# Retention in matmuls of 64 rows, one copy of queries and keys, and tails at other times, in a hybrid streaming encoder

## The chip, the core and the metric

The kernel runs on one core of a Trainium2 chip. A core has a matrix engine (TensorE, PE in the profile; its weight loads are listed as PEld), a vector engine (VectorE, DVE), an engine for activation functions (ScalarE, ACT), a general one (GpSimd, POOL), one that issues most DMAs here (SyncE, SP), an on-chip memory (SBUF) of 128 partitions, and eight accumulator banks for PE's results (PSUM), each of 512 fp32 numbers on 128 partitions. The metric is the device time of one execution in microseconds.

## What is computed

One layer over 2048 prompt tokens and 64 sample tokens, width 1024. The input is RMS-normalized and projected by one matrix; three groups of heads use parts of the projection, each result is multiplied by a SiLU gate, and one output projection with the residual and a final RMS norm follows.

```python
h = rms_norm(x, norm_g)
proj = h @ w_in
# q, f, i, gate of HGRN2 (8 heads, 128/128); q, k, v, gate of retention (4 heads, 64/128); q, gate of attention (4 heads, 128)
o_hg = head_rms_norm(hgrn2_chunkwise(...), hg_norm_g) * silu(hg_gate)
o_rt = head_group_norm(retention_chunkwise(rq, rk, rv, ...), rt_norm_g) * silu(rt_gate)
o_xa = softmax(xq @ mem_k) @ mem_v * silu(xa_gate)
y = final_norm(x + concat(o_hg, o_rt, o_xa) @ w_out)

# retention, per head, within a chunk and from the state R of the chunks before
scores = (q @ k.T) * gamma ** abs(n - m)
o = scores @ v + (q * gamma ** (pos + 1)) @ R
R = gamma ** chunk * R + (k * gamma ** (chunk - 1 - pos)).T @ v
# head_group_norm: subtract the mean over the head's 128 values, divide by the root of the mean square
```

A retention head has queries and keys of 64 numbers and values of 128, so that two heads' queries fill 128 partitions.

## The kernel before

Tokens are worked in two groups (0 to 1023; 1024 to 2047 and the 64 sample tokens), each in blocks of 256 to 512 tokens. Per group: the gates of the retention heads, then the retention (`v_group` projects the values, `ret_group` the queries and keys, 128 tokens at a time, `gemm_tok`, L294), then the HGRN2 heads in two halves, then the attention heads (`xa_heads`). Gated results go to `mixT` in device memory. At the end the output projection (L1189) reads `mixT` back in quarters of 512 features, 128 tokens at a time.

The large projections are kept accurate by splitting each fp32 operand into a high and a low part (`split`: ACT rounds the high part, L240; DVE subtracts it, L241) and by three single-pass matmuls in place of an fp32 one. The small matmuls of the heads, among them retention's, are plain fp32, each of which is two PE instructions in the trace.

PE's and SP's instructions run in the order in which the program emits them. That order is made by hand: the GEMM loops advance a virtual clock (`pe(us)`) and after each of eight steps call `poll()`. A *tail* is a generator given to `task(class, generator, delay)`; when the virtual clock has passed its due time, `poll` runs it to its next `yield d`, which makes it due again d us later. Tails of one class stay in order. So the constants `D_...` say how much GEMM work is put between the steps of a tail. DVE, ACT and POOL follow a scheduler that ranks instructions by where they are emitted, and tails get a bonus. A matmul that comes too early for its operand, or for its PSUM bank, makes PE stand, with all that is behind it.

One retention tile has these steps in `retention_tail` (before's lines):

- L629: PE transposes q and k of the 128 tokens (4 transposes, bank `tr`). L633, L634: ACT copies q into `q2`, a zero-padded matrix with two heads on a block diagonal; L637 copies k; L639: DVE makes q times its decay, all from the same bank.
- after `D_RT1` = 2.5: L646, scores of two heads in one matmul (128 rows of k for two heads, 256 columns of `q2`; bank `scb`), twice; L650: DVE multiplies by the decay table, 128x512; L656: four matmuls of k-decay with v, for the state's update, two heads side by side in the output's partitions.
- after `D_RT2` = 3.5: L662, q-decay times R (R is block diagonal, 256 columns), not for the first tile; L666: scores times v added in the same bank, `ob`; L675: DVE updates R; L682: sums for the mean; L686: subtraction of the mean; L691: ACT squares; L236, L237: POOL makes the power -1/2; L694: DVE multiplies by it; L698: SP loads the gate.
- after `D_RT3` = 6: L702, four transposes, and DVE multiplies by the gate; the result is stored 4.5 later.

The HGRN2 tail has the same last steps (L572 and L575 matmuls into `ob`, squares, POOL's power, L583 multiply, `D_HG3` = 4, L590 transposes). The attention tail of a head is emitted `D_XA0` = 4 after its query: L750 scores into `ob`, softmax (L754 to L764), transposes L772, L794 values.

PSUM's eight banks: three for GEMM accumulators (`acc`), two for transposes (`tr`), one for retention's scores (`scb`), two for head results (`ob`), used in turn. A bank is given again when its readers are through.

## Time and profile before

| What | Value |
|---|---|
| device time, median of 3 runs | 1924.35 us (1923.58 to 1924.72) |
| the profiled execution's own time | 1926.11 us |
| its span, first to last instruction | 1924.3 us |
| mean granted clock of PE | 0.994 of full speed |
| PE busy | 1890.8 us, 98% |
| DVE, ACT, POOL busy | 1079.4, 585.6, 143.8 us |

The profile gives the busy time of each engine. "Granted clock" is the speed that the chip's throttle left to PE, with 1 as full speed. The chain of work that ended last is followed back from the last instruction. A row of the timeline has the start, the length from the first start to the last end, the engine, the line in the code, the operation with the names of its result and operands, its tile of PE's array or its form, the count of instructions, and in brackets how long the engine had been idle and which instruction released it. Grouped rows have the busy time and the mean of one in ns behind a bar, then the idle time before them by its releaser. Window rows have the length, then busy time (with the number of instructions) of PE, PEld, DVE, ACT, POOL, then the granted clock, the DMA share and GB/s.

In the trace, the first group's retention lies between 140 and 215 us, the second's between 862 and 965 us, the first attention head's tail near 641 us, and the output projection from about 1542 us on.

### The profile page before, as it was taken

To read this page: it belongs to the slowest core of one execution; us is meant where nothing else is said; L and a number is where in the kernel's file an instruction comes from. 1 tells how busy PE (TensorE), PEld (TensorE's weight loads), DVE (VectorE), ACT (ScalarE), POOL (GpSimd) and SP (SyncE) were. 2 spreads that over 40 slices of the span, in tenths; PEclk is the share of its full clock that TensorE was granted. 3 is DMA by queue.
4 is the path that set the end of the run, shared out by engine and by line. 5 is a ranking of instruction groups with operands and counts; after the bars stand their busy time and mean duration, and the time that the engine had idled before them with its cause. 6 is when DMAs were issued, how large, how long until landed. Compare 5 with 4: busy or idle time off the path is not lost.

```text
span 1924.3 us, 28262 instructions
## 1 busy us (share of the span) xinstructions
PE 1890.8 (98%) x10938; PEld 1614.2 (84%) x10938; DVE 1079.4 (56%) x2672; ACT 585.6 (30%) x1414; POOL 143.8 (7%) x335
## 2 busy tenths in 40 slices
PE   8999999999999999999999999999999999999998
PEld 7888788888888787987789999899998978888886
DVE  8527458763778547416728886388865652222222
ACT  7412233322232434412323332233333431111111
POOL 0001100000100100001101111011100000000000
PEclk9999999999999999999999999999999999999999
DMA  7511212111111413411311111111222352223322
GB/s 256 180 59 49 82 55 61 56 44 50 45 48 58 155 54 118 132 46 52 96 55 47 50 49 53 44 50 50 60 61 75 107 172 89 88 88 108 111 72 61
DMA packets 116743, 153.22 MB, mean 80 GB/s; under 512 B 13312, under 2 KB 79232, under 8 KB 116608
## 3 DMA queue, kind: packets, MB, share of 16 engines
q1 hardware_dynamic: 116608, 151.41, 25.8%
q8 instruction: 86, 1.41, 0.3%
q14 instruction: 49, 0.40, 0.1%
HBM read 117.69 MB, written 33.69 MB: 79 GB/s over the span
## 4 chain that ended last, share of the span: by engine, by line
PE 87%; DVE 5%; DMA 2%; ACT 2%; issue 1%; POOL 1%; SPq 0%; DVEq 0%; POOLq 0%; ACTq 0%
PE acc L249 40%; PE acc L1189 19%; PE acc L294 15%; PE ob L540 2%; PE ob L572 2%; PE ob L575 1%; PE scb L523 1%; PE ob L750 1%; PE acc L794 1%; PE acc L264 1%; PE tr L516 1%; ACT s L691 1%; PE tr L772 1%; PE tr L590 1%; DVE r L675 1%
## 5 line engine op out<-in xcount | busy, mean ns | idle before, releaser
L249 PE MATMUL acc<-hb,whi 128*128 128x320 f32 (+2 forms) x1696 | 410.2, 332 | 0.4 <-DVE hb L371 0.4
L249 PE MATMUL acc<-ha,whi 128*128 128x512 f32 x1120 | 354.1, 397 | 0.0
L249 PEld LDWEIGHTS acc<-hb,whi 128*128 128x128 f32 x1696 | 285.0, 190 | 22.1 <-DVE hb L371 0.6
L241 DVE TENSOR_TENSOR wlo<-wst,whi 128x1024 fp32r<-128x1024 f32 x115 | 139.7, 1222 | 261.0 <-ACT whi L240 260.0
L249 PE MATMUL acc<-hb,wlo 128*128 128x256 f32 (+2 forms) x848 | 277.4, 327 | 0.0
L249 PEld LDWEIGHTS acc<-ha,whi 128*128 128x128 f32 x1120 | 204.2, 189 | 40.3 <-issue 1.6
L249 PE MATMUL acc<-ha,wlo 128*128 128x512 f32 x560 | 219.4, 392 | 0.0
L240 ACT CAST whi<-wst 128x1024 fp32r<-128x1024 f32 x115 | 119.7, 1051 | 209.4 <-PE acc L249 169.2
L249 PEld LDWEIGHTS acc<-hb,wlo 128*128 128x128 f32 x848 | 160.5, 189 | 11.3
L294 PE MATMUL acc<-whi,ha 128*128 128x512 f32 x512 | 161.5, 396 | 0.0
L294 PE MATMUL acc<-whi,hb 128*128 128x512 f32 x512 | 159.9, 394 | 0.0
L249 PEld LDWEIGHTS acc<-ha,wlo 128*128 128x128 f32 x560 | 105.2, 188 | 23.4 <-DVE wlo L241 0.2
L1189 PE MATMUL acc<-whi,s 128*128 128x512 f32 x396 | 123.2, 390 | 1.3 <-ACT s L240 1.0
L294 PEld LDWEIGHTS acc<-whi,hb 128*128 128x128 f32 x512 | 94.5, 188 | 19.6 <-issue 1.2
L294 PEld LDWEIGHTS acc<-whi,ha 128*128 128x128 f32 x512 | 94.0, 189 | 19.3 <-issue 1.0
L294 PE MATMUL acc<-wlo,ha 128*128 128x512 f32 x256 | 100.0, 391 | 0.0
L294 PE MATMUL acc<-wlo,hb 128*128 128x512 f32 x256 | 99.8, 390 | 0.0
L1189 PE MATMUL acc<-hb,s 128*128 128x512 f32 x400 | 95.1, 394 | 0.0
L241 DVE TENSOR_TENSOR s<-mst,s 128x512 fp32r<-128x512 f32 (+1 forms) x64 | 40.4, 672 | 97.4 <-ACT s L240 97.4
L1189 PE MATMUL acc<-ha,s 128*128 128x512 f32 x400 | 93.7, 389 | 0.0
L1189 PEld LDWEIGHTS acc<-hb,s 128*128 128x128 f32 x400 | 76.2, 191 | 15.9
L1189 PEld LDWEIGHTS acc<-whi,s 128*128 128x128 f32 x396 | 74.2, 188 | 17.0 <-ACT s L240 1.3
(237 smaller groups left out, 2944.6 us busy)
## 6 DMA issues: line engine op xcount, KB each, us to landing
wst<-w_in_t SPq DMA_DIRECT2D x104, 512.0 KB, 4.0
mixT<-s SPq DMA_DIRECT2D x64, 256.0 KB, 4.4
mst<-mixT SPq DMA_DIRECT2D x30, 512.0 KB, 5.8
wst<-w_out_t SPq DMA_DIRECT2D x16, 512.0 KB, 4.1
xq<-x_prompt SPq DMA_DIRECT2D x18, 256.0 KB, 5.1
o_yp<-xq SPq DMA_DIRECT2D x18, 256.0 KB, 2.2
s<-mixT SPq DMA_DIRECT2D x16, 256.0 KB, 3.1
s<-x_prompt SPq DMA_DIRECT2D x16, 256.0 KB, 4.7
```

Source lines behind the costliest of these rows:

```text
L240: S.copy(hi, src)
L241: V.tensor_tensor(out=lo, in0=src, in1=hi.bitcast(F32), op=ALU.subtract)
L249: T.matmul(ps[:, 0:nt], w[a][:, kk, :], ht[b][:, kk, 0:nt], start=(n == 0), stop=(n == 23))
L264: T.matmul(ps[:, 0:nt], w[a][:, kk, :], ht[b][:, kk, 0:nt], start=(kk == 0 and a + b == 0), stop=(kk == KT - 1 and a == 1))
L294: T.matmul(ps[0:L, :], ht[b][:, kk, o:o + L], w[a][:, kk % 2, :], start=(n == 0), stop=(n == 23))
L516: T.transpose(trk[:, c * 128:(c + 1) * 128], kch[:, c * 128:(c + 1) * 128], ident)
L523: T.matmul(scb[32 * j:32 * j + 32, c * 128 + 32 * e:(c + 1) * 128], K[:, c * 128 + 32 * e:c * 128 + 32 * e + 32], Qe[:, c, E_OFF[e]:E_OFF[ ...
L540: T.matmul(db[:, c * 128:(c + 1) * 128], kT[:, c * 128:(c + 1) * 128], vt[c], start=True, stop=True)
L572: T.matmul(ob[:, c * 128:(c + 1) * 128], A[:, c * 128:(c + 1) * 128], vt[c], start=True, stop=first)
L575: T.matmul(ob[:, c * 128:(c + 1) * 128], qst[:, c * 128:(c + 1) * 128], st[c][0], start=False, stop=True)
L590: T.transpose(tro[:, c * 128:(c + 1) * 128], on[:, c * 128:(c + 1) * 128], ident)
L1189: T.matmul(ps, m[a][:, kk % 4], w[b], start=(n == 0), stop=(n == 16 * len(terms) - 1))
```

## The change

1. Scores: two heads are no longer in one matmul with a zero-padded operand. Each head has its own matmul over 64 rows (partitions 0 to 63 or 64 to 127), 128 columns. The even heads' scores go to `scb`, the odd ones' to a second bank, from `ob`.
2. q-decay times R: the same, one matmul of 64 rows per head, between the two pairs of scores-times-v matmuls. Even and odd heads have a bank each, one from `acc`, one from `tr`. (The sample tile takes four matmuls over 128 rows.)
3. One ACT copy takes q and k together out of the transposes' bank; q times decay goes into the buffers that held the padded queries.
4. DVE's multiplication of the scores, the sums for the mean and the subtraction of the mean are two instructions each, one per bank.
5. In the retention and the HGRN2 tail, the multiplication by POOL's power is emitted `D_PW` = 2 later than the power; the step behind it comes correspondingly sooner after it, so that the sum of both delays stays.
6. Head 0's attention tail is due 6.5 instead of 4 after its query where the block starts at token 0 or 1024; the tail of the last tile of each group's retention starts 2 later.
7. The first two of the four quarters for the first output tile are split ahead of the gate projection of the last attention head.

```diff
 (constants)
+D_PW = 2.0
+D_XA00 = 6.5
 ...
 (HGRN2 tail)
         rsqrt_small(rs[:, 0:nch], ss[:, 0:nch], nch, 1.0 / 128, 4 * EPS)
+        yield D_PW
         V.tensor_tensor(...)
-        yield D_HG3
+        yield D_HG3 - D_PW
 ...
-            task("rt", retention_tail(...), D_RT0)
+            task("rt", retention_tail(...), D_RT0 + 2.0 * (last_tile and o + L == nt))
 ...
 (retention_tail)
         q2 = q2b[(t // 128) % 2]
-        S.copy(q2[0:64, :, 0:L], trv[0:64, 0:2, 0:L])
-        S.copy(q2[64:128, :, 128:128 + L], trv[64:128, 0:2, 0:L])
-        kq = slot()
-        kqv = kq.rearrange("p (a b) -> p a b", a=4)
-        S.copy(kqv[:, 0:2, 0:L], trv[:, 2:4, 0:L])
+        qk = slot()
+        qkv = qk.rearrange("p (a b) -> p a b", a=4)
+        S.copy(qkv[:, :, 0:L], trv[:, :, 0:L])
         if not first:
-            V.tensor_tensor(out=kqv[:, 2:4, 0:L], in0=trv[:, 0:2, 0:L], in1=qdec[:, :, 0:L], op=ALU.mult)
+            V.tensor_tensor(out=q2[:, :, 0:L], in0=trv[:, 0:2, 0:L], in1=qdec[:, :, 0:L], op=ALU.mult)
         yield D_RT1
+        sc2 = (scb, obank())
         for p in range(2):
 ...
-                T.matmul(scb[:, p * 256:(p + 1) * 256], kqv[:, p, :], q2[:, p, :], start=True, stop=True)
-            pe(0.426)
+            for hh in range(2):
+                sl = slice(64 * hh, 64 * hh + 64)
+                T.matmul(sc2[hh][0:L, p * 128:p * 128 + L], qkv[sl, 2 + p, 0:L], qkv[sl, p, 0:L], start=True, stop=True)
+            pe(0.3)
 ...
+        for hh in range(2):
+            V.tensor_tensor(out=sdv[0:L, hh:4:2, 0:L], in0=sc2[hh]..., in1=dtab..., op=ALU.mult)
 ...
         yield D_RT2
-        ob = obank()
-        for p in range(2):
-            if not first:
-                T.matmul(ob[0:L, p * 256:(p + 1) * 256], kqv[:, 2 + p, 0:L], R[:, p, :], start=True, stop=False)
-                pe(0.426)
+        ob2 = (acc(), trp())
+
+        def av(p, start, stop):
             for hh in range(2):
                 h = 2 * p + hh
-                T.matmul(ob[0:L, h * 128:(h + 1) * 128], sdv[0:L, h, 0:L], v[0:L, h * 128:(h + 1) * 128], start=first, stop=first or hh == 1)
+                T.matmul(ob2[hh][0:L, p * 128:(p + 1) * 128], sdv[0:L, h, 0:L], v[0:L, h * 128:(h + 1) * 128], start=start, stop=stop)
                 pe(0.213)
+
+        def qr(p, start, stop):
+            for hh in range(2):
+                sl = slice(0, P) if sample else slice(64 * hh, 64 * hh + 64)
+                T.matmul(ob2[hh][0:L, p * 128:(p + 1) * 128], q2[sl, p, 0:L], R[sl, p, 128 * hh:128 * hh + 128], start=start, stop=stop)
+            pe(0.3)
+
+        av(0, True, first)
+        if not first:
+            qr(0, False, True)
+            qr(1, True, False)
+        av(1, first, True)
 ...
         rsqrt_small(rs[0:L], ss[0:L], 4, 1.0 / 128, EPS)
+        yield D_PW
         V.tensor_tensor(out=ccv, in0=ccv, in1=bc(rs...), op=ALU.mult)
 ...
-        yield D_RT3
+        yield D_RT3 - D_PW
 ...
 (attention)
-        task("xa", att_tail(h, tok0, nt, kv_p, kv_s, qh, ql, sh), D_XA0)
+        task("xa", att_tail(h, tok0, nt, kv_p, kv_s, qh, ql, sh), D_XA0 if h or tok0 % 1024 else D_XA00)
         poll()
+        if h == 3 and tok0 + nt == NTOK:
+            y_early.extend(y_split(raw0[0:2], P))
         psg = gemm_col(wg, ht, nt, rel)
 ...
 (output projection)
+        m = y_early + y_split(raw[2:], L) if o == 0 else y_split(raw, L)
```

In the changed program the line numbers are higher: L294 becomes L296, L629 L632, L662 L671, L666 L665, L702 L716, L249 L251, L572 L574, L575 L577, L590 L593, L750 L766. The order of PE's instructions for one retention tile in the middle of the first group, with the score and state-update steps of the tile behind it, was this (a row is the line, operation, result and operands, form and count of matmuls):

```order
L629 MATMUL tr<-cst,s 128x128 x4
L294 MATMUL acc<-whi,hb_548 128x512
...
L662 MATMUL ob<-r_113,s 128x256
L666 MATMUL ob<-v,s 128x128 x2
L662 MATMUL ob<-r_113,s 128x256
L666 MATMUL ob<-v,s 128x128 x2
L702 MATMUL tr<-cst,s 128x128 x4
L646 MATMUL scb<-q2b_139,s 128x256 x2
L656 MATMUL ob<-v,s 64x128 x4
```

And this is the same place after the change:

```order
L632 MATMUL tr<-cst,s 128x128 x4
L665 MATMUL acc<-v,s 128x128
L665 MATMUL tr<-v,s 128x128
L671 MATMUL acc<-r_113,q2b_138 128x128
L671 MATMUL tr<-r_113,q2b_138 128x128
...
L716 MATMUL tr<-cst,s 128x128 x4
L296 MATMUL acc<-whi,hb_548 128x512
...
L646 MATMUL scb<-s 128x128
L646 MATMUL ob<-s 128x128
...
L657 MATMUL ob<-v,s 64x128 x4
```

The four L671 of a tile stand between two pairs of L665, and results go to `acc` and `tr`. At this tile the transposes L632 stand directly ahead of that block and L716 directly behind it; three GEMM matmuls, which stood ahead of the block, now follow it.

The second place is the attention tail of head 0 in the first group, on PE. `Sn` and `abuf` are operands of the HGRN2 tail before it, and L249/L251 is a column-wise GEMM. Before, from the last L575 to the HGRN2 transposes L590 (nine L249 stand between L575 and L750, six behind it):

```order
L575 MATMUL ob<-Sn,s 128x128
L249 MATMUL acc<-ha_454,whi 128x512
...
L750 MATMUL ob<-s 128x256 x12
L249 MATMUL acc<-ha_454,whi 128x512
...
L590 MATMUL tr<-cst,s 128x128 x4
```

After (21 L251 stand between L577 and L766):

```order
L577 MATMUL ob<-Sn,s 128x128
L251 MATMUL acc<-ha_454,whi 128x512
...
L766 MATMUL ob<-s 128x256 x12
L593 MATMUL tr<-cst,s 128x128 x4
```

The attention scores moved behind 12 more GEMM matmuls, and now stand directly ahead of the HGRN2 transposes.

The third place is ACT, about the sample tokens' GEMM in the second group (L275 folds that GEMM's result). Before:

```order
L240 CAST whi<-wst 128x1024 x4
L633 COPY q2b_139<-tr 64x2x128
L634 COPY q2b_139<-tr 64x2x128
L691 ACTIVATE s,ss_8130<-s 128x128 x4
L275 COPY s<-acc 64x512
L637 COPY s<-tr 128x256
```

After:

```order
L242 CAST whi<-wst 128x1024 x4
L704 ACTIVATE s,ss_8233<-s 128x128 x4
L277 COPY s<-acc 64x512
L638 COPY s<-tr 128x512
```

The queries' copies, which stood ahead of the squares, are part of one copy with the keys, behind the squares and the fold.

More of the change, by code (lines that the diff above doesn't have):

```diff
@@ L620, in retention @@
                             in1=bc(kdec[L][0:L].rearrange("p (h o) -> p h o", o=1), [L, 4, 64]), op=ALU.mult)
-            task("rt", retention_tail(t, L, vt[c], r, kd, R[0 if L == 128 else 1], dtab), D_RT0)
+            task("rt", retention_tail(t, L, vt[c], r, kd, R[0 if L == 128 else 1], dtab), D_RT0 + 2.0 * (last_tile and o + L == nt))
             poll()
@@ L632, in retention_tail @@
         q2 = q2b[(t // 128) % 2]
-        S.copy(q2[0:64, :, 0:L], trv[0:64, 0:2, 0:L])
-        S.copy(q2[64:128, :, 128:128 + L], trv[64:128, 0:2, 0:L])
-        kq = slot()
-        kqv = kq.rearrange("p (a b) -> p a b", a=4)
-        S.copy(kqv[:, 0:2, 0:L], trv[:, 2:4, 0:L])
+        qk = slot()
+        qkv = qk.rearrange("p (a b) -> p a b", a=4)
+        S.copy(qkv[:, :, 0:L], trv[:, :, 0:L])
         if not first:
-            V.tensor_tensor(out=kqv[:, 2:4, 0:L], in0=trv[:, 0:2, 0:L], in1=qdec[:, :, 0:L], op=ALU.mult)
+            V.tensor_tensor(out=q2[:, :, 0:L], in0=trv[:, 0:2, 0:L], in1=qdec[:, :, 0:L], op=ALU.mult)
         yield D_RT1
+        sc2 = (scb, obank())
         for p in range(2):
-            if sample:
-                for hh in range(2):
-                    T.matmul(scb[0:L, p * 256 + hh * 128:p * 256 + hh * 128 + L], kqv[:, p, 0:L], q2[:, p, hh * 128:hh * 128 + L], start=True, stop=True)
-            else:
-                T.matmul(scb[:, p * 256:(p + 1) * 256], kqv[:, p, :], q2[:, p, :], start=True, stop=True)
-            pe(0.426)
+            for hh in range(2):
+                sl = slice(64 * hh, 64 * hh + 64)
+                T.matmul(sc2[hh][0:L, p * 128:p * 128 + L], qkv[sl, 2 + p, 0:L], qkv[sl, p, 0:L], start=True, stop=True)
+            pe(0.3)
         sd = slot()
         sdv = sd.rearrange("p (a b) -> p a b", a=4)
-        V.tensor_tensor(out=sdv[0:L, :, 0:L], in0=scb.rearrange("p (a b) -> p a b", a=4)[0:L, :, 0:L],
-                        in1=dtab.rearrange("p (a b) -> p a b", a=4)[0:L, :, 0:L], op=ALU.mult)
+        for hh in range(2):
+            V.tensor_tensor(out=sdv[0:L, hh:4:2, 0:L], in0=sc2[hh].rearrange("p (a b) -> p a b", a=4)[0:L, 0:2, 0:L],
+                            in1=dtab.rearrange("p (a b) -> p a b", a=4)[0:L, hh:4:2, 0:L], op=ALU.mult)
         db = obank()
@@ L681, in retention_tail @@
         mu = small(4, "mu")
-        V.tensor_reduce(out=mu[0:L], in_=ob[0:L].rearrange("p (a b) -> p a b", a=4), axis=AX.X, op=ALU.add)
+        for hh in range(2):
+            V.tensor_reduce(out=mu[0:L, hh:4:2], in_=ob2[hh][0:L, 0:256].rearrange("p (a b) -> p a b", a=2), axis=AX.X, op=ALU.add)
         V.tensor_scalar(out=mu[0:L], in0=mu[0:L], scalar1=1.0 / 128, scalar2=None, op0=ALU.mult)
@@ L685, in retention_tail @@
         ccv = cc[0:L].rearrange("p (a b) -> p a b", a=4)
-        V.tensor_tensor(out=ccv, in0=ob[0:L].rearrange("p (a b) -> p a b", a=4),
-                        in1=bc(mu[0:L].rearrange("p (a o) -> p a o", o=1), [L, 4, 128]), op=ALU.subtract)
+        for hh in range(2):
+            V.tensor_tensor(out=ccv[:, hh:4:2, :], in0=ob2[hh][0:L, 0:256].rearrange("p (a b) -> p a b", a=2),
+                            in1=bc(mu[0:L, hh:4:2].rearrange("p (a o) -> p a o", o=1), [L, 2, 128]), op=ALU.subtract)
         ss = small(4, "ss4")
@@ L1039, in layer_kernel, with y_split @@
     order = list(range(0, SEQ - P, P)) + [SEQ, SEQ - P]
-    def y_load(o, raw):
-        L = 128 if o < SEQ else DEC
-        src = io["x_prompt"][0, o:o + L] if o < SEQ else io["x_sample"][0]
-        if order.index(o) % 2:
-            x = a_buf
-        else:
-            xq = qep.tile([P, 4, 320], F32, tag="Qe", name="xq").rearrange("p a b -> p (a b)")
-            x = [xq[:, 0:512], xq[:, 512:1024]]
+    y_early = []
+    def y_split(raw, L):
         m = []
@@ L1058, in y_load @@
             m.append((hi, lo))
+        return m
+    def y_load(o, raw):
+        L = 128 if o < SEQ else DEC
+        src = io["x_prompt"][0, o:o + L] if o < SEQ else io["x_sample"][0]
+        if order.index(o) % 2:
+            x = a_buf
+        else:
+            xq = qep.tile([P, 4, 320], F32, tag="Qe", name="xq").rearrange("p a b -> p (a b)")
+            x = [xq[:, 0:512], xq[:, 512:1024]]
+        m = y_early + y_split(raw[2:], L) if o == 0 else y_split(raw, L)
         for i in range(2):
```

## The prediction

> **What bounds the kernel now.** I read the page first: busy time by engine, and the chain of work that ended last.
>
> ```profile
> span 1924.3 us, 28262 instructions
> PE 1890.8 (98%) x10938; PEld 1614.2 (84%) x10938; DVE 1079.4 (56%) x2672; ACT 585.6 (30%) x1414; POOL 143.8 (7%) x335
> PE 87%; DVE 5%; DMA 2%; ACT 2%; issue 1%; POOL 1%; SPq 0%; DVEq 0%; POOLq 0%; ACTq 0%
> s<-mixT SPq DMA_DIRECT2D x16, 256.0 KB, 3.1
> ```
>
> TensorE (PE) is busy 98% of the span and carries 87% of the chain. So two things move the end: PE's own work, and the few places where PE stands. Those are the second view, PE's waits by line (total us, times, longest; a line is that of the instruction, "<-" the one it waited for).
>
> ```profile
> PE tr L629 <- DVE s L617: 2.9, 2, 1.8
> PE scb L646 <- ACT s L637: 2.7, 1, 2.7
> PE acc L794 <- DVE s L241: 2.4, 2, 2.0
> PE tr L772 <- DVE s L764: 2.3, 1, 2.3
> PE ob L750 <- DVE s L583: 2.2, 1, 2.2
> PE tr L702 <- DVE s L694: 1.4, 2, 0.8
> PE ob L750 <- DVE Sn L563: 1.0, 1, 1.0
> PE acc L1189 <- ACT s L240: 1.0, 1, 1.0
> PE ob L656 <- DVE r L675: 0.6, 1, 0.6
> ```
>
> The third view is the granted clock by stretch. Behind a PE wait of over 2 us the clock falls to half for 3.4 us; the longer stretches hold one such fall each.
>
> ```profile
> 943.60:947.00 3.40, 3.40 (x17) 2.33 (x16) 2.84 (x6) 0.00 (x0) 0.46 (x1) 0.50 1.07 356
> 635.00:650.00 15.00, 12.64 (x64) 10.62 (x63) 6.08 (x17) 8.31 (x31) 3.95 (x11) 0.89 0.57 198
> 738.00:752.00 14.00, 11.69 (x50) 9.29 (x49) 12.59 (x24) 7.49 (x17) 0.00 (x0) 0.89 0.38 110
> 1538.00:1568.00 30.00, 26.34 (x132) 21.75 (x131) 21.14 (x39) 17.50 (x36) 0.00 (x0) 0.95 0.70 215
> 140.00:215.00 75.00, 71.23 (x406) 57.53 (x404) 54.52 (x114) 21.99 (x85) 8.62 (x14) 1.00 0.30 81
> ```
>
> The column after the five engines is the clock. Lost work is (1 - clock) x length: 3.4 x 0.50 = 1.7 us behind the 2.7 us wait, 15 x 0.11 = 1.65 behind the 2.2 us one at L750, 1.5 behind L772, 1.5 behind L794. So such a stall costs its length and about 1.6 us more. The last row is the retention of the first group: clock 1.00, VectorE (DVE) idle for 20 of 75 us.
>
> **Matmuls of 64 rows.** The timeline of PE inside one retention tile gives the spacings.
>
> ```profile
> 143.70 1.02 PE L646 MATMUL scb<-q2b,s 128*128 128x256 f32 x4
> 144.66 0.66 PE L656 MATMUL ob<-v,s 128*64 128x128 f32 x8
> 145.24 0.73 PE L294 MATMUL acc<-whi,ha 128*128 128x512 f32 x2
> 145.81 0.39 PE L294 MATMUL acc<-wlo,ha 128*128 128x512 f32 x1
> 146.93 0.39 PE L294 MATMUL acc<-wlo,ha 128*128 128x512 f32 x1
> 149.23 1.05 PE L666 MATMUL ob<-v,s 128*128 128x128 f32 x8
> 203.46 0.59 PE L662 MATMUL ob<-r,s 128*128 128x256 f32 x2
> 203.89 0.61 PE L666 MATMUL ob<-v,s 128*128 128x128 f32 x4
> ```
>
> An fp32 matmul is two PE instructions. A new one starts every (203.89-203.46)/2 = 0.215 us at 256 moving columns; about 0.27 us of each row's length is the drain of its last instruction. L666, 128 columns, full array: (1.05-0.27)/7 = 0.111 us apart. L656, also 128 columns but on half the array's output columns each: (0.66-0.27)/7 = 0.056. So two half-array matmuls do run at once in this program, for column halves. Row halves occur nowhere in this trace.
>
> Going into a half mode and out again costs: from 143.70 to 145.81 are 2.11 us, of which 4 x 0.215 + 8 x 0.055 + 2 x 0.23 = 1.76 is work (0.23 is a GEMM matmul of 512 columns: 10 start from 146.93 to 149.23). That leaves 0.35 for two switches, 0.18 each.
>
> Scores per tile: now 2 matmuls x 2 x 0.215 = 0.86 us. Then 4 matmuls of 128 columns, two at once: 4 x 0.11 = 0.44, and one switch more (row halves stand between full and column halves): 0.62, so -0.24 on 16 prompt tiles = -3.8. q·R: now 0.86, then 0.44 and two switches = 0.80, -0.06 on 15 tiles = -0.9. I take -4.5. Ends: row halves run one after another, and only the switches are added: 16 x 0.18 + 15 x 0.36 = +8.3. Both overlap and the switches vanish in weight loads: 31 x -0.43 = -13.3. I take the overlap because L656, the nearest row, is the same engine split the other way.
>
> [...]
>
> **One copy, halves on DVE, powers apart.** These rows are of the first group's retention, with the ACT copies.
>
> ```profile
> 146.68 0.37 ACT L633 COPY q2b<-tr 64x256 f32<-64x256 f32 x1 [4.39 <-PE tr L629]
> 728.91 0.59 ACT L361 COPY s<-tr 128x512 f32<-128x512 f32 x1 [3.73 <-PE tr L357]
> L694 DVE TENSOR_TENSOR s<-s,rs 128x512 f32<-128x512 f32 x7 | 4.8, 693 | 11.4 <-POOL rs L237 11.4
> L639 DVE TENSOR_TENSOR s<-tr,cst 128x256 f32<-128x256 f32 x7 | 2.9, 420 | 2.3 <-ACT s L637 2.3
> L675 DVE SCALAR_TENSOR_TENSOR r<-r,cst,ob 64x128 f32<-64x128 f32 x24 | 7.6, 343 | 0.1
> ```
>
> Three ACT copies of 0.37 (1.11) become one of 0.59: transposes to scores gets 0.5 us shorter. Three DVE operations on 128x512 (L650's scores, the reduction, the subtraction; 0.69 as L694) become pairs on 128x256 (0.42 as L639): +0.15 each, +0.45 us a tile, covered by the 20 us of idle. The normalizing multiply now stands in DVE's queue waiting for POOL's power, 11.4/7 = 1.6 us a tile, and everything behind it waits too (the q·decay multiply, r updates, weight splits). Two us of schedule between power and multiply take that wait out, so DVE's net is about -1.2 us a tile. The gate's DMA goes on SP's queue 2 us later as well, and weight fetches pass it; it lands in 3.1 us and has 4 left. The sample tile keeps four full matmuls; it is not counted.
>
> What PE waits in the retention, L646 aside, is 2.9 + 1.4 + 0.6 = 4.9 us, nearly all on DVE. Against that, the second half of each result now takes a transpose bank, of which there are two. So every tile passes that ring three times (L632, L665/L671, L716). Counting matmuls in the order (0.23 us for each of the GEMM's), 7 of the 17 tiles have only 1.3 to 2.9 us of PE work between the transposes and the next user of a bank that DVE or ACT must clear; DVE needs 4 x 0.34 + 4 x 0.42 = 3 us for updates, sums and subtractions. Ends: all 4.9 go, or 7 tiles wait 1 us each and the old waits stay, +7. I take -1, near the middle, as a quicker DVE and a busier ring oppose each other.
>
> **The wait before the sample tile** stands at 939.8 to 942.9.
>
> ```profile
> 941.92 0.56 ACT L275 COPY s<-acc 64x512 f32<-64x512 f32 x1
> 942.51 0.37 ACT L637 COPY s<-tr 128x256 f32<-128x256 f32 x1
> 942.93 1.47 PE L646 MATMUL scb<-q2b,s 128*128 128x256 f32 x4 [2.73 <-ACT s L637]
> ```
>
> ACT's order after the change still has the squares and the fold copy L275 ahead of the one copy; it ends at best 0.5 earlier, and PE's work ahead changes little. -0.5, the slow stretch stays. If other work comes ahead of it on PE, up to -2.7 - 1.7 = -4.4; if the 0.59 copy is late, +0.2.
>
> **Moved tails.** The attention tail behind head 0 and the HGRN2 tails:
>
> ```profile
> 643.51 1.65 PE L750 MATMUL ob<-s 128*128 128x256 f32 x6 [2.22 <-DVE s L583]
> 642.77 0.69 DVE L583 TENSOR_TENSOR s<-ob,rs 128x512 f32<-128x512 f32 x1 [2.38 <-POOL rs L237]
> 748.06 1.03 PE L772 MATMUL tr<-cst,s 128*128 128x128 f32 x6 [2.31 <-DVE s L764]
> 744.14 2.35 DVE L241 TENSOR_TENSOR wlo<-wst,whi 128x1024 fp32r<-128x1024 f32 x2
> 1560.89 1.14 ACT L240 CAST v<-wst 128x512 fp32r<-128x512 f32 x2 [2.42 <-DMA wst<-w_out_t]
> ```
>
> First head: L750 wants a bank that L583 clears, and L583 waits for the power. In the new order 21 instead of 9 GEMM matmuls stand between, 12 x 0.23 = 2.8 us later, which is over the 2.22 of the wait: -2.1, and its slow stretch -1.65, so -3.7. Head 0 of token 1024 passes the state work in the same way: -1, the whole of L563's wait. At 748.1 the order has DVE do L764 ahead of the two 1.2 us splits, but PE arrives 6 matmuls (1.4 us) earlier: -0.7 (ends 0 and -3.8). The multiply of the HGRN2 tail pushes its transposes one poll back, 0.7 us of GEMM between; hidden. Output stage: two of its first four splits are done beforehand, -1, the whole of L1189's wait; the wait at L794 hangs on the late w_out fetch (2.42) ahead of ACT's casts and stays.
>
> **Sum.** -4.5 - 1 - 0.5 - 3.7 - 1 - 0.7 - 1 = -12.4 us. The profiled execution took 1926.11, 1.8 above the median of the runs; the sum is a difference, so against the median: 1924.35 - 12.4 = 1912.
>
> **Rivals.** 1. *Row halves don't overlap* (the part that wouldn't do what it says): each half has its own 128-column weight load, and L656 overlapped loads of 64 columns only; L666 never shows 128-column loads nearer than 0.111. Then 4 x 0.22 = 0.86 a block as before, plus switches, +8.3 in place of -4.5: 1912 + 12.8 = 1925. For it: no row-half row at all; against: L656.
>
> [...]
>
> 2. *The stalls move*: the bank at the first head is waited for by the next user, the clock falls there all the same, the output stage waits for its third quarter instead. Then only the rows (-4.5), the retention (-1) and head 0 of token 1024 (-1) count: 1918. For it: POOL's power itself is not earlier; against: 12 matmuls cover it.
>
> 3. *The transpose ring binds* (slower): L716 or L632 meets a bank that DVE hasn't cleared, because a pair of splits of 2.35 us stands in DVE's queue. At 7 tight places of 2.35 us each, +16.5, and a stall of that length has drawn a slow stretch of 1.6 each time; with two of them more, +20. 1912 + 1 + 20 = 1933. Slower than before from (12.4 - 1 + 3.85)/7 = 2.2 us a place on. Against it: DVE loses its 1.6 us waits.
>
> **Chances.** The forecast 0.5, its own range 1905 to 1918; rival 1, 0.18; rival 2, 0.2; rival 3, 0.12. A difference under 0.2% (3.85 us) can't be told from none: same is 1920.5 to 1928.2. Forecast and rival 2 are faster but for 0.04 at the edge of it; rival 1 is the same, at 0.16, with 0.02 slower; rival 3 is slower. Faster 0.66, same 0.20, slower 0.14. The range goes from 1903 (the rows' term at its low end: 1912 - 13.3 + 4.5) to 1926, just over rival 1, leaving out rival 3 and little below.
>
> **What would show it.** Rows of 64: L646 and L671 should be about 0.055 us apart in the timeline; 0.11 proves rival 1. The idle ahead of L750's successor at 641 and ahead of the first L1189 successor gone, clock at 635 to 650 near 1.00. DVE's idle behind POOL at the two multiplies (11.4 us for seven) near 0. Waits of L632 and L716 on DVE of 2 us would be rival 3. The prediction fails outright if the first retention stage (75 us in the last window row) is not shorter by 2 us or more, or if a new wait over 2 us draws a slow clock.

## The result, and the profile after

The changed kernel takes 1912.05 us (median of 4 runs, 1909.42 to 1914.49) where the kernel before, in 4 runs, takes 1923.96: a ratio of 0.994 [0.9927, 0.9952]. A second measurement gave 0.9936 [0.9923, 0.9948]. The forecast was 1912, and the time is right. Most of its terms are of the right kind too, but their sizes are not, so that the sum is right by luck. Within about 2 us the gain comes from the moved delays, and not from the matmuls of 64 rows, which the forecast had as its largest term.

The page of the changed kernel (span; busy time by engine; the chain):

```profile
span 1907.6 us, 28493 instructions
PE 1882.3 (99%) x11066; PEld 1607.2 (84%) x11066; DVE 1081.8 (57%) x2723; ACT 576.3 (30%) x1380; POOL 144.2 (8%) x335
PE 87%; DVE 6%; DMA 2%; ACT 2%; issue 1%; POOL 1%; SPq 0%; POOLq 0%; DVEq 0%; ACTq 0%
```

PE is still the bound: busy for 8.5 us less (1890.8 before) in a span that is 16.7 us shorter. So half of what went from this profiled execution is standing time, and of the 8.5 about 3.4 are two stretches of slow clock fewer, in which matmuls take longer (in the kernel before, those of 512 columns start 0.43 us apart at half clock, 645.81 to 646.24 us, and 0.23 apart at full clock). (This execution, 1909.42 us, was the fastest of its kernel's four, and the one shown of the kernel before, 1926.11, was slower than all four timed beside it; that is why the spans differ by more than the 12 us of the medians.)

PE's waits after the change:

```profile
PE ob L766 <- DVE s L586: 3.1, 2, 2.1
PE tr L716 <- DVE s L708: 2.5, 4, 1.2
PE acc L810 <- DVE s L243: 2.4, 2, 1.7
PE scb L646 <- ACT s L638: 2.4, 1, 2.4
PE tr L632 <- DVE s L620: 1.4, 1, 1.4
```

L772's wait (now L788), the first L1189's (L1211) and L656's are gone from the head of the list. The attention scores (L766) still wait twice for the bank that L586 clears, once near 641 us as before and once at 1411 us, where L750 had waited 1.0 for something else. The transposes L716 wait more often.

The stretch at the first attention head now has a clock of 1.00, and so has the piece behind it; the one at the sample tile keeps its slow stretch ((1 - 0.88) x 14 = 1.7 us lost), and so does the output stage (the last row):

```profile
635.00:650.00 15.00, 14.04 (x71) 11.74 (x70) 6.85 (x16) 10.09 (x35) 4.62 (x13) 1.00 0.34 112
730.00:744.00 14.00, 14.00 (x73) 11.88 (x72) 13.84 (x28) 8.30 (x20) 0.00 (x0) 1.00 0.22 53
926.00:940.00 14.00, 11.56 (x77) 8.89 (x77) 11.04 (x23) 4.29 (x13) 2.15 (x2) 0.88 0.68 207
1522.00:1552.00 30.00, 27.61 (x141) 23.47 (x141) 22.18 (x42) 17.80 (x36) 0.00 (x0) 0.94 0.72 218
```

And these are the scores of a retention tile on PE, with the GEMM matmuls around them:

```profile
141.34 0.39 PE L296 MATMUL acc<-wlo,ha 128*128 128x512 f32 x1
141.66 0.37 PE L646 MATMUL scb<-s 64*128 64x128 f32 x1
141.66 0.37 PE L646 MATMUL ob<-s 64*128 64x128 f32 x1
141.87 0.27 PE L646 MATMUL scb<-s 64*128 64x128 f32 x1
141.88 0.27 PE L646 MATMUL ob<-s 64*128 64x128 f32 x1
141.98 0.27 PE L646 MATMUL scb<-s 64*128 64x128 f32 x1
141.99 0.27 PE L646 MATMUL ob<-s 64*128 64x128 f32 x1
...
142.30 0.66 PE L657 MATMUL ob<-v,s 128*64 128x128 f32 x8
142.89 0.72 PE L296 MATMUL acc<-whi,ha 128*128 128x512 f32 x2
143.45 0.39 PE L296 MATMUL acc<-wlo,ha 128*128 128x512 f32 x1
```

The two halves start within 0.01 us of each other: they run at once, and rival 1 is out. The first pair takes 0.21 us, the others 0.11 (the fourth, at 142.09, is left out above). From the end of the GEMM's matmul (141.34 + 0.23) to the next one at 142.89 are 1.32 us; before, 143.70 to 145.24 were 1.54. So a tile's scores save 0.22 us.

To see where time went I set the k-th projection matmul of one trace against the k-th of the other: these matmuls are the same in all versions, and the difference of their times, stage by stage, is what a stage gained or lost. Differences to the profiled execution before, in us; the stages are placed by the times of the kernel before. Slow stretches of the clock are 3.41 us at a granted clock of 0.50 in all traces (but for the one that runs into the program's end, of 6.55 us in the kernel before), or two or three of these in a row, each of which loses 3.41 x 0.50 = 1.7 us; in brackets stands how many more or fewer of them the stage has than before.

```
kernel        start     ret.1     635-850   ret.2     1417-30   output    all
after         -2.3      -1.8      -8.5 (-2) -3.0      +0.6      -1.8      -16.8
after_again   -1.3 (-1) -1.5      -9.0 (-2) -1.1 (+1) +0.6      -1.7      -14.0
rows_only      0.0 (-1) +0.3 (+1) -1.6      +2.3 (+2)  0.0      -0.2       +0.6
pw_only       -0.1 (-1)  0.0      -2.8 (-1) -0.2      -0.3      +0.1       -2.9
xa_only       -1.1       0.0      -5.3 (-1) +1.1      +2.1 (+1) +0.9       -2.4
y_only        -1.4 (-1)  0.0      -2.9 (-2) +2.0 (+2)  0.0      -3.1 (-1)  -5.5
sched_only    -0.7      -0.6      -9.3 (-2) -1.2      +0.6      -3.2 (-1) -14.1
rt_no_pw      -1.6 (-1) -0.1 (+1) -8.7 (-2) -2.3      +2.1 (+1) -3.2 (-1) -13.7
```

(Retention lies from 149 to 224 and from 851 to 966 us, the output stage's beginning from 1543 to 1633. What is missing to the sum lies between the stages, under 0.6 us each.) Single executions of a program differ by 1 to 2 us in a stage: the start by 1.0 between the two of the changed kernel, and the second retention by 1.1 between the kernel before and `xa_only`, whose retention is the same. So the start's 2.3 us are not shown to be the change's: in the second profile it is 1.3, and a missing slow stretch makes 1.7 of that.

The mean granted clock of every timed execution is on record as well. Its time times (1 - clock) is what it lost to the clock. Where "lost to the clock" and "the rest" are given below, they are means over all executions of a kernel; a difference of two such means is good to 1 to 2 us unless said otherwise.

### The profile page after: what moved, and what is told of

Read it like the earlier page. It is cut to its first block, busy times and chain, and to the rows that moved or that the text cites. A ratio compares the mean times of both kernels' runs of the same rounds, so it can differ in the third digit from the quotient of the medians.

```text
span 1907.6 us, 28493 instructions
## 1 busy us (share of the span) xinstructions
PE 1882.3 (99%) x11066; PEld 1607.2 (84%) x11066; DVE 1081.8 (57%) x2723; ACT 576.3 (30%) x1380; POOL 144.2 (8%) x335
## 4 chain that ended last, share of the span: by engine, by line
PE 87%; DVE 6%; DMA 2%; ACT 2%; issue 1%; POOL 1%; SPq 0%; POOLq 0%; DVEq 0%; ACTq 0%
PE acc L251 40%; PE acc L1211 18%; PE acc L296 15%; PE ob L542 2%; PE ob L574 1%; PE ob L577 1%; PE scb L525 1%; PE acc L810 1%; PE ob L766 1%; PE acc L266 1%; POOL rs L239 1%; PE tr L518 1%; PE tr L788 1%; ACT s L704 1%; PE tr L593 1%
## 5 line engine op out<-in xcount | busy, mean ns | idle before, releaser
L251 PE MATMUL acc<-hb,whi 128*128 128x320 f32 (+2 forms) x1696 | 409.0, 331 | 0.4 <-DVE hb L373 0.4
L251 PE MATMUL acc<-ha,whi 128*128 128x512 f32 x1120 | 353.0, 396 | 0.0
L251 PEld LDWEIGHTS acc<-hb,whi 128*128 128x128 f32 x1696 | 284.4, 189 | 22.0 <-DVE hb L373 0.6
L251 PE MATMUL acc<-hb,wlo 128*128 128x256 f32 (+2 forms) x848 | 276.9, 326 | 0.0
L251 PEld LDWEIGHTS acc<-ha,whi 128*128 128x128 f32 x1120 | 204.1, 188 | 40.5 <-issue 1.3
L251 PE MATMUL acc<-ha,wlo 128*128 128x512 f32 x560 | 219.1, 391 | 0.0
L251 PEld LDWEIGHTS acc<-hb,wlo 128*128 128x128 f32 x848 | 160.1, 189 | 11.2
L296 PE MATMUL acc<-whi,ha 128*128 128x512 f32 x512 | 161.4, 396 | 0.7 <-ACT v L1100 0.7
L296 PE MATMUL acc<-whi,hb 128*128 128x512 f32 x512 | 160.0, 394 | 0.0
L251 PEld LDWEIGHTS acc<-ha,wlo 128*128 128x128 f32 x560 | 105.1, 188 | 23.3 <-DVE wlo L243 0.2
L1211 PE MATMUL acc<-whi,s 128*128 128x512 f32 x396 | 122.9, 389 | 0.0
L296 PEld LDWEIGHTS acc<-whi,ha 128*128 128x128 f32 x512 | 93.9, 189 | 20.5 <-issue 1.2
L296 PEld LDWEIGHTS acc<-whi,hb 128*128 128x128 f32 x512 | 94.5, 188 | 19.6 <-issue 1.2
L296 PE MATMUL acc<-wlo,ha 128*128 128x512 f32 x256 | 100.0, 391 | 0.0
L296 PE MATMUL acc<-wlo,hb 128*128 128x512 f32 x256 | 99.9, 390 | 0.0
L1211 PE MATMUL acc<-hb,s 128*128 128x512 f32 x400 | 94.9, 393 | 0.0
L1211 PE MATMUL acc<-ha,s 128*128 128x512 f32 x400 | 93.7, 389 | 0.0
L1100 ACT COPY v<-acc 128x512 f32<-128x512 f32 x48 | 28.1, 586 | 204.4 <-PE acc L296 204.4
L1211 PEld LDWEIGHTS acc<-hb,s 128*128 128x128 f32 x400 | 76.0, 190 | 15.9
```

What stands on the lines that cost most here:

```text
L251: T.matmul(ps[:, 0:nt], w[a][:, kk, :], ht[b][:, kk, 0:nt], start=(n == 0), stop=(n == 23))
L296: T.matmul(ps[0:L, :], ht[b][:, kk, o:o + L], w[a][:, kk % 2, :], start=(n == 0), stop=(n == 23))
L1100: S.copy(v, ps)
L1211: T.matmul(ps, m[a][:, kk % 4], w[b], start=(n == 0), stop=(n == 16 * len(terms) - 1))
```

## The experiments

Each was timed in five rounds beside the kernel before, and profiled once. Ratios are to the kernel before. First the two halves of the change.

**Rows alone** (`rows_only`): all edits of the retention's matmuls, copies and DVE halves; none of the delays.

```diff
 (the changed kernel, less)
-        yield D_PW                     # both tails; D_HG3, D_RT3 whole again
-  ... D_RT0 + 2.0 * (last_tile and o + L == nt)
-  ... D_XA0 if h or tok0 % 1024 else D_XA00
-            y_early.extend(y_split(raw0[0:2], P))
```

> The kernel before with matmuls of 64 rows, the one copy and the halved DVE instructions, and no delay moved. If the row halves overlap as priced (a pair every 0.11 us, switches 0.18), it gains 4.5 us, and about 1 in the retention's waits: ratio 0.997, some 1918.5 us where the kernel before takes 1924; the waits at the first attention head (2.2 us and the slow stretch behind it) and behind it at 745 us stay. If the moved tails are the whole gain and the switches eat the overlap, 1923 to 1925, ratio 0.999 to 1.001.

Measured: 1925.97 us, 1.001 [0.9998, 1.0022]. No gain. The blocks on PE are as short as in the changed kernel, yet the retention stages are 0.3 and 2.3 us longer, with one and two slow stretches more. The 12 executions agree: 14.6 us are lost to the clock, where the kernel before, beside them, loses 9.3, while the rest is 3.3 us shorter (1911.4 against 1914.7). So most of what the rows save on PE does arrive, and slow stretches take it back. PE's waits there, of `rows_only`, first in the first group, then in the second:

```profile
PE acc L664 <- DVE s L650: 3.0, 1, 3.0
PE tr L631 <- DVE s L619: 0.5, 1, 0.5
...
PE tr L631 <- DVE q2b L639: 2.4, 1, 2.4
PE scb L645 <- ACT s L637: 2.3, 1, 2.3
PE tr L631 <- DVE s L619: 1.8, 1, 1.8
PE ob L656 <- DVE s L650: 0.6, 1, 0.6
```

The 3.0 us are a wait for the scores' multiplication (L650), which the kernel before did not have. Its timeline, around 203 us:

```profile
202.58 0.69 DVE L706 TENSOR_TENSOR s<-s,rs 128x512 f32<-128x512 f32 x1 [1.32 <-POOL rs L239]
203.19 0.42 DVE L650 TENSOR_TENSOR s<-scb,s 128x256 f32<-128x256 f32 x1
203.53 0.41 DVE L650 TENSOR_TENSOR s<-ob,s 128x256 f32<-128x256 f32 x1
203.75 0.48 PE L664 MATMUL acc<-v,s 128*128 128x128 f32 x2 [3.00 <-DVE s L650]
```

DVE works its queue in order here. The normalizing multiply of the tile before stands in it; DVE is idle for 1.32 us until POOL has the power, and only then come the scores that PE is waiting for, although their last matmul had started at 195.58 us. In the first group this only gathers the standing in one place: 3.7 us in sum with the small waits, where the kernel before stood 3.8 (L629's 1.8, L702's 1.4, L656's 0.6). But behind the 3.0 us a slow stretch follows at 204.1 us, and its 1.7 us are what the scores of the group's eight tiles save (8 x 0.22). In the second group PE also stands longer, 7.3 us against 4.6, and two more slow stretches follow.

**Delays alone** (`sched_only`): the kernel before with 128-row matmuls, and all four moves in time.

```diff
+D_PW = 2.0
+D_XA00 = 6.5
+        yield D_PW                     # both tails, taken off D_HG3 and D_RT3
+  ... D_RT0 + 2.0 * (last_tile and o + L == nt)
+  ... D_XA0 if h or tok0 % 1024 else D_XA00
+            y_early.extend(y_split(raw0[0:2], P))
```

> The kernel before with the moved delays alone (multiply 2 us behind its power, head 0's attention tail at 6.5, the last retention tail 2 later, the early split), and 128-row matmuls. By the sum of the prediction (-3.7 - 1 - 0.7 - 1, and some of the retention's waits) 1917 to 1918, ratio 0.9965. If the moved tails are the whole gain: 1912, ratio 0.994.

Measured: 1911.15 us, 0.9931 [0.9919, 0.9943], the same as the whole change; the rest is 8.0 us shorter, and 4.8 instead of 9.3 us are lost to the clock. So the rival wording, that the moved tails are the whole gain, is what holds within about 2 us. In the profile the changed kernel's retention is 0.9 to 1.2 us shorter than `sched_only`'s in the first group, and in the second 1.8 shorter in one execution and 0.1 longer in the other; in the total the difference disappears in the spread.

**Retention's multiply behind its power again** (`rt_no_pw`).

```diff
         rsqrt_small(rs[0:L], ss[0:L], 4, 1.0 / 128, EPS)
-        yield D_PW
 ...
-        yield D_RT3 - D_PW
+        yield D_RT3
```

> The changed kernel without the 2 us between power and multiply in the retention tail (HGRN2's stays). If the 3.8 us that the 64-row matmuls save on PE are only kept because DVE does not stand behind POOL there, the two retention stages get 4 to 7 us longer in sum: 1915 to 1918. If the early rows_only loss came from elsewhere: 1910 to 1912.

Measured: 1916.51 us, 0.9954 [0.9941, 0.9967], beside the changed kernel's 1911.04 (0.9936) in the same comparison; the intervals just overlap. The timeline is plainer. The wait of `rows_only` is back, at the same tile, for the same instruction, and a slow stretch follows it at 203.2 us:

```profile
201.06 0.69 DVE L707 TENSOR_TENSOR s<-s,rs 128x512 f32<-128x512 f32 x1 [1.32 <-POOL rs L239]
201.67 0.42 DVE L651 TENSOR_TENSOR s<-scb,s 128x256 f32<-128x256 f32 x1
202.24 0.46 PE L665 MATMUL acc<-v,s 128*128 128x128 f32 x2 [2.99 <-DVE s L651]
```

The multiply behind POOL's power, in DVE's queue ahead of the scores, is the cause of this wait: it comes and goes with this one delay. The standing in the stage is not longer for it, 3.4 us in sum as against 3.2 and 3.4 in the two profiles of the changed kernel, because the waits of L716 there (2.3 us) are down to 0.2. What the stage loses, 1.4 to 1.7 us (-0.1 against -1.5 and -1.8), is the slow stretch. The second retention is not clearly longer, so that the 4 to 7 us expected of the two stages are not seen in the profile; but this execution, 1912.33 us, was the fastest of its five. Over the executions 10.7 us are lost to the clock, against 6.5 in `after_again`, and the rest is 0.8 us shorter, the first good to 3 us and the second to 2. As far as these means go, the delay's worth lies in the clock rather than in shorter waits.

**Two halves that do not alternate** (`halves_in_turn`).

```diff
-        for p in range(2):
-            for hh in range(2):
+        for hh in range(2):
+            for p in range(2):
                 T.matmul(sc2[hh]..., qkv[sl, 2 + p, 0:L], qkv[sl, p, 0:L], ...)
```

> The changed kernel with the four score matmuls of a tile in another order: both of the upper 64 rows, then both of the lower, so that neighbours in the queue use the same rows. If the overlap of two row halves is the gain of that part, most of it is lost: a tile's block goes from 0.44 to up to 0.8 us, +4 to +6 us over 16 tiles, 1916 to 1918. If the overlap is not what counts, no change: 1912, within 1.5 us.

Measured: 1909.93 us, 0.9922 [0.9908, 0.9935], no loss. The experiment missed its aim, and shows why in its timeline:

```profile
142.04 0.37 PE L646 MATMUL scb<-s 64*128 64x128 f32 x1
142.05 0.37 PE L646 MATMUL ob<-s 64*128 64x128 f32 x1
142.25 0.27 PE L646 MATMUL scb<-s 64*128 64x128 f32 x1
142.27 0.27 PE L646 MATMUL ob<-s 64*128 64x128 f32 x1
```

Both matmuls of the upper rows (`scb`, four instructions) stand in the queue ahead of the lower ones (`ob`), but the records put the first `ob` 0.01 us behind the first `scb`. (The trace shows starts and not the queue; its order is that of the program's text.) The overlap was not taken away, so its worth is known only from the block lengths above.

**q times R over all rows** (`qr_full`).

```diff
-                sl = slice(0, P) if sample else slice(64 * hh, 64 * hh + 64)
+                sl = slice(0, P)
                 T.matmul(ob2[hh]..., q2[sl, p, 0:L], R[sl, p, 128 * hh:128 * hh + 128], ...)
```

> The changed kernel with q times R in matmuls over all 128 rows (the other head's rows of R are zero), four of 128 columns per tile, in the same place and banks. By the price of the prediction the row halves save only 0.06 us a tile there, because two switches of 0.18 eat the 0.42 of overlap: +0.9 us, 1912 to 1914, not to be told from none. If the switches are hidden, +0.43 a tile, +6.5 us: 1918.5.

Measured: 1908.66 us, 0.9918 [0.9907, 0.993]: nothing lost. Its block of q times R and scores times v, and then that of the changed kernel, first and last instruction and the next:

```profile
153.29 0.38 PE L665 MATMUL acc<-v,s 128*128 128x128 f32 x2
154.84 0.39 PE L665 MATMUL tr<-v,s 128*128 128x128 f32 x2
```

```profile
153.09 0.38 PE L665 MATMUL acc<-v,s 128*128 128x128 f32 x2
154.82 0.38 PE L716 MATMUL tr<-cst,s 128*128 128x128 f32 x2
```

In `qr_full`, 154.84 is the last pair of 16 instructions at 0.111, so the next starts at 155.06, 1.77 behind the first. With row halves it is 1.73. The row halves of q times R are worth 0.04 us a tile by these blocks (0.02 against the kernel before, whose block at such a place takes 1.75). That is what overlap less two switches was forecast to leave, nearly nothing.

**Each delay by itself**, on the kernel before.

```diff
+        yield D_PW                     # pw_only: both tails
```

> The kernel before with only the multiply 2 us behind its power, in both tails; head 0's tail at 4 as before, no early split. If the later tail of head 0 (6.5) is what removed the waits at 641 and 745 us, the two waits of 2.2 and 2.3 us with their slow stretches stay, and only some 2 us in the retention go: 1921 to 1922. If the multiply that no longer holds up DVE's queue removed them: 1914 to 1916.

```diff
+  ... D_XA0 if h or tok0 % 1024 else D_XA00     # xa_only
```

> The kernel before with head 0's attention tail at 6.5 instead of 4 for tokens 0 and 1024, and nothing else. If this one delay is what took the waits at 641 and 745 us and their two slow stretches away, as the stage table of the runs so far suggests (multiply and power apart gave nothing by themselves), 1915 to 1918, ratio 0.996. If it needs the multiply apart from its power as well: 1921 to 1925.

```diff
+            y_early.extend(y_split(raw0[0:2], P))     # y_only
```

> The kernel before with the early split of two quarters alone. By the prediction -1 (the wait at the first output matmul): 1923. By the traces of the runs with it, where the output stage began 1.7 to 3.3 us earlier, the larger figure when no slow stretch followed: 1921 to 1922, ratio 0.9985.

Measured: `pw_only` 1925.4, 1.0005 [0.9996, 1.0014]; `xa_only` 1923.21, 0.9994 [0.9983, 1.0005]; `y_only` 1920.49, 0.9987 [0.9975, 0.9998]. On 1924 us these are +1.0, -1.2 and -2.5, in sum -2.7, each about 2 us either way; together with the last tile's delay, which was not run alone, they give -13.3. That one acts in the retention stages, where `sched_only` gains 1.8 at most. So the theories by which one delay carries the gain fall, the multiply's and head 0's alike. The 10.6 us that are missing are about half waits and half clock: the rest is 8.0 us shorter in `sched_only` and 3.0 in the three together, and 4.5 us less are lost to the clock, against none.

One place shows how the delays hang together. `pw_only` keeps the waits at 641 and 745 us as they were (2.22 and 2.32 us). `xa_only` takes both away, but stands 25 us behind the first. Its ACT and PE:

```profile
667.14 0.63 ACT L313 ACTIVATE s<-s 128x512 f32<-128x512 f32 x1 [3.60 <-DMA s<-x_prompt]
668.41 0.63 ACT L313 ACTIVATE s<-s 128x512 f32<-128x512 f32 x1 [0.55 <-DMA s<-x_prompt]
669.04 0.56 ACT L241 CAST s<-tr 128x512 fp32r<-128x512 f32 x1
669.66 0.50 PE L795 MATMUL acc<-s 128*128 128x512 f32 x1 [0.82 <-ACT s L241]
```

ACT stands 3.60 us for an input of the next group, with the squares L313, and behind it in its queue is the cast of the second half of the attention's transposes that PE needs; the transposes themselves had started at 662.32 us. PE waits in four pieces, the longest of 0.82, and a slow stretch follows at 672.2. In `sched_only` the casts stand ahead of that:

```profile
663.77 1.07 ACT L242 CAST s<-tr 128x512 fp32r<-128x512 f32 x2
665.76 0.64 ACT L314 ACTIVATE s<-s 128x512 f32<-128x512 f32 x1
```

From 663 to 693 us `xa_only` takes 4.5 us longer than `sched_only`. The order of ACT there is another where all the delays are moved. That it is the multiply's delay that moves it is likely, as the other two act elsewhere, but not shown: no run has just the multiply's and head 0's. How the rest of the 10.6 us falls on the stages stays open: the single profiles carry chance stretches (`y_only` lacks two where it changes nothing) of the same size.

`y_only` gains more than the wait it was priced at: its output stage is 3.1 us shorter, of which one slow stretch makes 1.7 and the waits 1.4.

**Three versions beyond the change.** `tuned_b` and `tuned_c` put head 0 of token 1024 behind 18 GEMM matmuls; `tuned_a` has besides a delay before the last prompt tile's scores, `tuned_c` besides q times R over all rows.

```diff
-  ... D_XA0 if h or tok0 % 1024 else D_XA00
+  ... D_XA0 if h or tok0 % 1024 else D_XA00 if tok0 == 0 else 9.5     # all three
-        yield D_RT1
+        yield D_RT1 + (2.0 if t + P == SEQ else 0.0)                  # tuned_a
```

> The changed kernel with two delays moved: head 0 of token 1024 at 9.5 instead of 6.5 (18 GEMM matmuls, 4.1 us, between the state matmuls and the attention scores, against the wait of 2.1 us at 1411 us), and 2 us more between the transposes and the scores of the last prompt tile (9 GEMM matmuls, 2.1 us, against the wait of 2.4 us with its slow stretch at 930 us). If these waits are only a matter of PE's order: -2.1 and -2.1 to -4.1, 1905 to 1908. If ACT or DVE are late for another reason there and the wait moves: 1909 to 1912.

> The changed kernel with head 0 of token 1024 at 9.5 instead of 6.5, and nothing else. The run with a second delay showed this place 2.4 us shorter than the changed kernel: 1908 to 1910, ratio 0.9925. If the wait comes back at the next user of the bank: 1911 to 1912.

> The same, and q times R over all 128 rows. If the row halves of q times R save next to nothing (0.02 us a tile by the blocks in the trace) this equals the run beside it, 1908 to 1910; if leaving them out helps, as 1908.7 against 1912 suggested, 1906 to 1907, ratio 0.991.

And the changed kernel again, as their measure:

> The changed kernel unaltered, as the measure for the other three runs beside it. 1909 to 1913 by its earlier runs; if the first 45 us of its profile again lie 2 us below those of the kernel before, that gain belongs to the change, else to the spread between executions.

Measured: `tuned_a` 1909.59, 0.9924 [0.991, 0.9937]; `tuned_b` 1909.37, 0.9929 [0.9914, 0.9945]; `tuned_c` 1909.41, 0.9926 [0.991, 0.9942]; `after_again` 1911.04, 0.9936 [0.9923, 0.9948]. In all three the place at 1420 us is 2.4 us shorter than in the changed kernel (-1.8 against +0.6 in the terms of the table). The delay at the last prompt tile, in `tuned_a`, only moved its wait, now to the transposes, as the second reading of its expectation had it:

```profile
PE tr L716 <- DVE s L708: 4.8, 5, 2.2
PE acc L810 <- DVE s L243: 2.8, 2, 2.1
PE tr L632 <- DVE s L620: 2.6, 1, 2.6
```

All three beat the kernel before. Against the changed kernel the lead of 1.5 us is inside the intervals, and cannot be told from none.

## Why the prediction was right, and where it was not

- **Rows, -4.5.** Row halves overlap, a pair every 0.11 us, and what is left over at a switch is about what was priced. From the end of the GEMM's matmul at 141.57 to the second one behind the scores, at 143.45, are 1.88 us; four pairs of scores (0.44), the eight instructions of L657 (8 x 0.055 = 0.44) and two GEMM matmuls (0.46) leave 0.54 for three switches, 0.18 each, as priced. The block of q times R leaves 1.73 - 12 x 0.111 = 0.40 for two. -0.22 us a tile for the scores was forecast as -0.24, -0.02 to -0.04 for q times R as -0.06: 16 x 0.22 + 15 x 0.04 = 4.1 us of PE's work at most. The step that failed is to count that as time gained, with no price for the clock. PE arrives earlier at banks and scores that DVE clears no earlier, waits gather (one of 3.0 us in the first group), and slow stretches follow (three more in the two stages): alone the rows make the rest 3.3 us shorter and lose 5.3 us more to the clock (1.001 in all), and beside the delays they give nothing that the measurements of the total can tell.
- **Retention's waits, -1.** Net 4.9 to 3.9 us in the changed kernel (L632's 1.4 and L716's 2.5; 4.6 in its second profile), about as forecast, but not for the forecast reason. DVE's idle behind POOL, which should have gone to near 0, is almost as long:

```profile
L708 DVE TENSOR_TENSOR s<-s,rs 128x512 f32<-128x512 f32 x6 | 4.2, 692 | 7.9 <-POOL rs L239 7.9
```

  7.9/6 = 1.3 us a tile instead of 1.6. What changed is what stands behind it in the queue; `rows_only` shows the bad case.
- **Sample tile, -0.5, slow stretch stays.** 2.7 to 2.4 us, and it stayed. Right.
- **First head, -3.7, and 748 us, -0.7.** Together -4.4 forecast, -8.5 to -9.0 measured from 635 to 850 us. Two slow stretches make 3.4 of it, the waits 5.1 to 5.6. Near 641 about 1 us of the 2.22 stays (the smaller of L766's two waits, 3.1 - 2.1): 2.8 us more of GEMM did not cover all of it, because the power also came later (6.1 us behind the start of the last state matmuls, 5.0 before). In the second profile 0.4 stays. The place at 748 us was mis-sized: the wait of 2.3 went altogether, with its slow stretch; and a wait near 702 us (L750 for ACT's L240), which I had not priced, went too. I had weighed PE's earlier arrival above DVE's order; DVE's order was what counted (L780 at 735.97 us, the split at 737.70).
- **Token 1024, -1.** Wrong: +0.6. The scores passed the state matmuls with no GEMM between, and then waited for the bank that the norm of just those matmuls clears:

```profile
1410.97 0.56 DVE L586 TENSOR_TENSOR s<-ob,rs 128x384 f32<-128x384 f32 x1 [0.79 <-POOL rs L239]
1411.59 0.97 PE L766 MATMUL ob<-s 128*128 128x256 f32 x6 [2.13 <-DVE s L586]
```

  It is the wait of the first head, in a new place; `tuned_b` takes it away with 18 matmuls.
- **Output stage, -1.** -1.7 and -1.8 in the two profiles of the changed kernel, -3.1 and -3.2 where a slow stretch was missing as well. Right in kind, small by 0.7 to 2 us.
- **Sum.** -12.4 forecast, -11.9 measured by the medians. That it agrees is luck: the rows' -4.5, of which nothing is seen in the total, and the lost -1 at token 1024 stood against 4 to 5 us too little at the first head and behind it, and 1 to 2 too little in the output stage.
- **The rivals.** 1 is out by the timeline. 2, that the waits move to the next user, came true for `xa_only`, not for the whole. 3, DVE as the bound of the retention, is what `rows_only` shows, through the queue behind POOL as well as through the transpose ring (L631's 2.4 us for L639): its price there is the rows' gain, given back, and more of it to the clock than to the waits. In the changed kernel the ring costs L716's 2.5 us, in four places of 1.2 at most, below the 2.2 a place from which it would have decided.
- **Its own signs.** The pairs came as named, and so did the clock of 1.00 at 635 to 650 us. DVE's idle behind POOL did not go. By one of its two signs of failing outright the prediction failed: the first retention stage had to be 2 us shorter, and is 1.8 and 1.5 in the table, which is near enough to it that the spread between executions could decide. The other, a new wait over 2 us with a slow clock, is the wait at 1411 us (2.13): none in the two profiles of the changed kernel, one in `qr_full`, `rt_no_pw` and `xa_only`.
- **Overlap and switches.** The pairs of a tile's scores start 0.21, 0.11 and 0.11 us apart; with 0.11 for the last they make a block of 0.54 us, where 0.44 was forecast. The 0.10 more of the first pair are counted above among the switches. Of q times R 0.04 us of the gain is left beside two switches, where 0.06 was forecast. A switch is here what is left of a block when its matmuls are taken off; what PE does in that time no run shows. The 0.27 us that the prediction calls the drain of the last instruction are the length of one record of 128 columns (L666: 275 ns, the median); one of 256 columns is 379 ns long (L662, the mean).

## What to carry to other kernels

Where one engine is busy 98% and waits for few things, as here, shorter work on it brings it earlier to what others must clear. Price the cleared bank beside the matmul, and the slow stretch that a wait gathered in one place can draw: here the 1.7 us lost behind one wait of 3.0 us took back what 64 rows saved in the first group. An instruction that waits in a queue worked in order made everything behind it wait here (a multiply 1.32 us behind its power, squares 3.60 us behind a DMA), so look at what stands behind before removing it. Moves in time work together: three that changed the time by +1, -1 and -2.5 us alone gained 13 with one more beside them, and trying them singly would have dropped two.

## What was not expected of the hardware

That a slow stretch follows a PE wait of over 2 us held at the places the prediction read it from (2.73, 2.22, 2.31 and 2.0 us in the kernel before), but not in `y_only`: the wait's length alone does not decide it. In the kernel before, the waits of 2.22 and 2.31 us were followed by one each. In `y_only`, with those two places untouched, the same waits were not:

```profile
642.07 0.98 PE L752 MATMUL ob<-s 128*128 128x256 f32 x6 [2.21 <-DVE s L583]
745.19 1.03 PE L774 MATMUL tr<-cst,s 128*128 128x128 f32 x6 [2.31 <-DVE s L766]
```

And a wait of 2.13 us at 1411 us drew none in the changed kernel, and one in `qr_full`, whose wait there is also 2.13 (clock of 1409 to 1419 us: 1.00 and 0.83).

The traces show most of what decides here. In the kernel before, stretches of 3.413 us at a clock of 0.50 begin at 643.22, 749.03, 943.59 and 1564.82 us, which is 31, 57 and 182 times 3.413 us apart; in the changed kernel at 930.01 and 1547.83, 181 times. Within each of the traces all slow stretches but the one at the program's end begin and end whole multiples of 3.413 us apart, so that they lie on a grid. From the span's start its first line is at 1.51 us in the kernel before, at 1.58 in the changed kernel and at 2.74 in `y_only`. These are pieces of that grid, three of `y_only` and one of the kernel before:

```profile
637.62:641.03 3.41, 1.96 (x11) 1.30 (x9) 0.69 (x1) 3.41 (x17) 2.41 (x6) 1.00 0.93 315
641.03:644.44 3.41, 2.37 (x14) 2.06 (x15) 2.18 (x5) 0.55 (x4) 1.15 (x4) 1.00 0.27 101
743.43:746.84 3.41, 1.65 (x10) 1.41 (x11) 3.41 (x8) 1.91 (x3) 0.00 (x0) 1.00 0.92 243
639.80:643.22 3.42, 1.36 (x8) 0.83 (x6) 1.04 (x2) 2.73 (x14) 2.47 (x7) 1.00 0.89 294
```

What PE's column, the first behind the length, lacks of 3.41 us is standing. In `y_only` the first wait falls on two pieces, with 1.45 and 1.04 us of standing, and the second has 1.76 in its piece; in the kernel before 2.06 and 2.31 us lie in one piece each. At 1411 us it is 1.83 in the changed kernel and 2.13 in `qr_full`. I call a piece slow when its clock is half. Over all 14 traces, without the first 12 us, the program's end and pieces that are slow themselves: 31 pieces have 1.88 us of standing or more, and the next piece is slow each time (four of them in the kernel before, with 2.04 to 2.73, one in the changed kernel, with 2.36); 7657 have under 1.65, and the next is slow once; of the 14 between, five are followed by a slow one (in the changed kernel the piece at 1544.41 us with 1.70 is, the one at 1407.88 with 1.83 is not). So the same wait, 2.31 us near 745 us, cost 1.7 us more in the kernel before and nothing in `y_only`, where the grid lay otherwise. Five or six waits of about 2 us come to 8.5 to 10 us that way, an estimate from the 1.7 us of each; the 23 executions of the kernel before that were timed beside `y_only` lie from 1918.76 to 1928.76 us. A single profile's total says little about 0.3%. For this kernel the counts say to keep PE's standing within one piece of 3.41 us under 1.65. Why a slow stretch at times goes on for two or three pieces stays open: at the sample tile, behind the same wait of 2.7 us, it was 3.41 us in the kernel before and 10.24 in `y_only`.

The second: matmuls on the lower rows started 0.01 us behind those on the upper ones though the second matmul of the upper rows stood between them in the program (`halves_in_turn`).
